# Attention heads: weight splits queued behind the scores' exponentials, and the remainders of eleven weights made by an accumulating transfer

## Chip, cores and metric

One core of one Trainium2 chip runs the kernel. The metric is the device time of one execution in microseconds (us). The engines are TensorE (PE; its weight loads are shown as PEld), VectorE (DVE), ScalarE (ACT), GpSimd (POOL) and SyncE (SP), each with a queue of its own that is worked off in order.

## Reference

Two layers on a sequence of 512 tokens of width 1024: a Mamba-2 layer with an FFN, then multi-head attention with an FFN. The change is in the attention layer, eight heads over four blocks of 128 queries:

```python
c_q = rms_norm(h @ q_down, q_norm_g)
q = (c_q @ q_up).reshape(b, s, MLA_N_HEADS, MLA_NOPE + MLA_ROPE)
...
scores = (jnp.einsum('bqhd,bkhd->bhqk', qn, k_nope)
          + jnp.einsum('bqhr,bkr->bhqk', qr, k_rope)).astype(jnp.float32) * scale
...
scores = jnp.where(key_idx[None, :] <= q_idx[:, None], scores, -jnp.inf)
p = jax.nn.softmax(scores, axis=-1).astype(v.dtype)
return jnp.einsum('bhqk,bkhd->bqhd', p, v)
...
return o @ out_proj
```

## The kernel before

**Splits.** Every product is made in fp32 accuracy from two parts of each operand: a rounded part and the remainder. `WStream` streams all weights in the order of use. `load` (line 54) puts one weight tile into a buffer `wst`; `_split` makes `wh` from it by a copy on ScalarE (line 96) and `wl = wst - wh` by a subtraction on VectorE (line 97). A product takes three passes: `wh` with the rounded activations, `wl` with them, `wh` with their remainders. `wh` and `wl` have six buffers each, `wst` six. `ahead(i, most)` splits up to `most` tiles beyond item i. The attention's items are, at the end of the list, `hw` 0 to 7 (one tile of 640 columns per head, q and k weights together) and `ow` 0 to 7 (output weights, 1024 columns).

**One pass of the head loop** (in `mla`, for h from 0 to 7) issues, in this order of code: `qk(h + 1)`, the q and k products of the next head, whose two banks ScalarE casts (line 1235, `qT`, `kT`) and VectorE takes the remainders of (line 1236); for every second head `qk_rope(h + 1)`, four transposes into one bank, which gives `qrT` of two heads, `qrT0` and `qrT1` below (cast at line 1251, remainder at line 1252; the second cast waits for the first remainder); one split; `pv(h - 1)`, whose bank becomes `oT` (lines 1307, 1308); `ptrans(h)`, ten transposes of the probabilities `E` into four banks, from which `PT` is cast (line 1290) and its remainder taken (line 1291); one more split; `scores(h + 1)`, four blocks i = 0 to 3 of 128, 256, 384 and 512 columns, each with five products in one bank (line 1265), the mask (1273), the maximum (1275), the exponential on ScalarE (1277), and the reciprocal and scaling on VectorE (1278, 1279). "Head h" is below the stretch that begins with `qk(h)` and ends with `scores(h)`, so that it holds `pv(h - 2)` and `ptrans(h - 1)`, and the exponentials that ScalarE runs during it are those of head h - 1.

**What sets the order.** A scheduler orders the queues of all engines but SP from the order of the code and its own estimate of times; `tc.issue_after(x)` keeps what is issued inside it behind x. The result is fixed when the kernel is built, and the chip works each queue off in that order. The eight PSUM banks (`k.bank()`) go round: a bank is given again eight requests later, and TensorE's first product into it waits until the last engine has read it. In a head with `qk_rope` the requests are q, k, rope, pv, four of `ptrans`, four of `scores`: block 2 of the scores gets the bank of `qk_rope`, block 3 that of `pv`. In a head without it block 3 gets the bank of `pv` likewise, and block 2 that of k.

Of the kernel before, what the change touches and what calls it, by code (L numbers as in the profile page):

```python
# [13 lines left out]
AF = mybir.ActivationFunctionType  # L14
ALU = mybir.AluOpType
# [3 lines left out]
P = 128  # L19
# [9 lines left out]


class WStream:

# [41 lines left out]
    def _split(self, nst=None):  # L76
        nc = self.k.nc
        i = self.split
        f, kind, part = (self.items[i][1:] + (None, None))[:3]
        if kind == "=":  # L80
            self.st[i] = self.st["+"]
        elif i not in self.st:
            self.load(i)
        s = self.st.pop(i)
        if kind == "+":
            self.st["+"] = s
            r = self.sums[part]
            nc.vector.tensor_tensor(r[:, :f], r[:, :f], s[:, :f], op=ALU.add)  # L88
            s = r
        elif kind == "-":  # L90
            nc.vector.tensor_tensor(s[:, :f], self.sums[part][:, :f], s[:, :f], op=ALU.subtract)
        if kind not in ("r", "a", "+"):
            self.out -= 1
        h = self.k.wh.tile([P, 1024], F32R, name="wh")
        l = self.k.wl.tile([P, 1024], F32R, name="wl")
        nc.scalar.copy(h[:, :f], s[:, :f])  # L96
        nc.vector.tensor_tensor(l[:, :f], s[:, :f], h[:, :f], op=ALU.subtract)  # L97
        self.w[i] = (h, l)
        self.split += 1
        self.fill(nst)  # L100
# [956 lines left out]
AH, QR, KVR, RD = 8, 384, 256, 64  # L1057
SCALE = (128 + 64) ** -0.5
# [6 lines left out]
def mla_items(dw, vw, rw, hw, ow):  # L1065

    it = [(dw[j], 1024) for j in range(4)] + [(dw[j][:, :768], 768) for j in (4, 5)]
    rv = rw.rearrange("(k p) n -> p k n", p=P)
    it += [(rv[:, 0:2, :], 1024), (rv[:, 2:3, :], 512)]
    vv = vw.rearrange("(k p) n -> p k n", p=P)  # L1070
    it += [(vv[:, :, hf * 512:(hf + 1) * 512], 1024) for hf in range(2)]
    it += [(hw[h], 640) for h in range(AH)]
    it += [(ow[j * P:(j + 1) * P, :], 1024) for j in range(AH)]
    return it


# [45 lines left out]
def mla(k, ws, base, ngp, gb):  # L1122
    nc, tc = k.nc, k.tc
    with ExitStack() as cx:
# [16 lines left out]
        n = [base]  # L1141
# [84 lines left out]
        def qk(h, off=0):  # L1226
            S = H.setdefault(h, {})
            w = [v[:, :640].rearrange("p (k m) -> p k m", k=5) for v in ws.get(n[0] + off, 0)]
            bq, bk = k.bank(), k.bank()
            k.mm_a(bq, [v[:, 0:3] for v in w], cT[:3], slice(0, SEQ))  # L1230
            k.mm_a(bk, [v[:, 3:5] for v in w], cT[3:], slice(0, SEQ))

            for nm, b, sc in (("q", bq, SCALE), ("k", bk, 1.0)):
                t = one.tile([P, 2, SEQ], F32R, name=f"{nm}T")
                a = nc.scalar.activation(t[:, 0], b, AF.Copy, scale=sc)
                d = nc.vector.scalar_tensor_tensor(t[:, 1], b, sc, t[:, 0], op0=ALU.mult, op1=ALU.subtract)
                S[nm] = t
            if not off:
                ws.retire(n[0])
                n[0] += 1  # L1240
            return a, d

        def qk_rope(h):
            if h % 2 == 0:
                b = k.bank()
                for i in range(NT):
                    nc.tensor.transpose(b[:, i * P:(i + 1) * P], qr[:, i, h * RD:(h + 2) * RD], k.ident)
                for e in range(2):
                    t = one.tile([P, SEQ], F32R, name=f"qrT{e}")
                    s = b[e * RD:(e + 1) * RD, :]  # L1250
                    a = nc.scalar.activation(t[:RD], s, AF.Copy, scale=SCALE)
                    d = nc.vector.scalar_tensor_tensor(t[RD:], s, SCALE, t[:RD], op0=ALU.mult, op1=ALU.subtract)
                    H.setdefault(h + e, {})["r"] = t
                return a, d

        def scores(h):
            S = H[h]
            S["E"] = []
            for i in range(NT):
                b = k.bank()  # L1260
                L = (i + 1) * P
                qs = slice(i * P, L)
                o = b[:, :L]
                q, kk, r = S["q"], S["k"], S["r"]
                mm = lambda l, m, s, e: nc.tensor.matmul(o, l, m, start=s, stop=e, skip_group_check=True)  # L1265
                mm(q[:, 0, qs], kk[:, 0, :L], True, False)
                mm(q[:, 0, qs], kk[:, 1, :L], False, False)
                mm(q[:, 1, qs], kk[:, 0, :L], False, False)
                mm(r[:, qs], ka[:, :L], False, False)
                mm(r[:, qs], kb[:, :L], False, True)  # L1270

                d = b[:, qs]
                nc.vector.tensor_tensor(d, d, mask, op=ALU.add)
                m = two.tile([P, 4], F32, name="smx", bufs=4)
                nc.vector.tensor_reduce(m[:, 0:1], o, axis=AX.X, op=ALU.max, negate=True)  # L1275
                e = one.tile([P, L], F32, name=f"E{i}")
                nc.scalar.activation(e, o, AF.Exp, bias=m[:, 0:1], accum_out=m[:, 1:2])
                nc.vector.reciprocal(m[:, 2:3], m[:, 1:2])
                nc.vector.tensor_scalar(e, e, m[:, 2:3], None, op0=ALU.mult)  # L1279
                S["E"].append(e)  # L1280

        def ptrans(h):
            S = H[h]
            S["P"] = []
            for j in range(NT):
                b = k.bank()
                for i in range(j, NT):
                    nc.tensor.transpose(b[:, i * P:(i + 1) * P], S["E"][i][:, j * P:(j + 1) * P], k.ident)
                t = one.tile([P, 2, SEQ - j * P], F32R, name=f"PT{j}")
                a = nc.scalar.copy(t[:, 0], b[:, j * P:])  # L1290
                d = nc.vector.tensor_tensor(t[:, 1], b[:, j * P:], t[:, 0], op=ALU.subtract)  # L1291
                S["P"].append(t)
            return a, d

        def pv(h):
            S = H.pop(h)
# [54 lines left out]
        n[0] += 3  # L1351
        for h in range(AH):
            if h + 1 < AH:

                ends = qk(h + 1)
                a, d = qk_rope(h + 1) or ends
                with tc.issue_after(a.ins), tc.issue_after(d.ins):
                    ws.ahead(n[0], most=1)
            else:
                k.load_ln(gb)  # L1360
                out_piece(0, 2, 0, ALPHA, False)
            if h:
                pv(h - 1)
            a, d = ptrans(h)
            if h + 1 < AH:
                with tc.issue_after(a.ins), tc.issue_after(d.ins):
                    ws.ahead(n[0], most=1)
            if h + 1 < AH:
                scores(h + 1)
        for i in range(1, NT):  # L1370
            out_piece(0, 2, i, ALPHA, False)
        pv(AH - 1)
# [90 lines left out]
```

## Time and profile before

| | us |
|---|---|
| median of 3 runs | 1312.35 (1311.97 to 1312.97) |
| the profiled execution's own time | 1311.7 |
| its span, first to last instruction | 1310.0 |
| busy in the span: PE, PEld, DVE | 1299.5, 1098.9, 1020.6 |
| busy in the span: ACT, POOL | 636.0, 93.1 |

TensorE is busy nearly everywhere by this table, but a product that waits inside its pipeline counts as busy, so stalls of some tenths of a microsecond are read from the waits and from the starts of its instructions. The granted clock of TensorE was 0.998 of full speed (the upper level, 2.4 GHz) over the span.

### The profile page before, as it was taken

The page shows a single profiled execution, that of the slowest core. Times are in us where ns is not written, and L with a number is a line of the kernel's source. Part 1 is how long each engine was busy: PE and PEld are TensorE (multiplying, and loading weights), DVE is VectorE, ACT ScalarE, POOL GpSimd, SP SyncE. Part 2 cuts the span into 40 slices and gives each one's busy share as a digit, 9 for nine tenths or more (in the row PEclk, how much of TensorE's full clock was granted, in tenths as well). Part 3 has the DMA queues.
Part 4 walks back from the last instruction along what each step waited for, and adds up shares of the span by engine and source line. Part 5 has one row for each costly group of instructions (what it writes and reads, how often), then busy time and mean ns, then how long its engine had stood idle before and what let it go on. Part 6 is the DMA issues. An engine that isn't in the chain of part 4 may idle for free.

```text
span 1310.0 us, 17422 instructions
## 1 busy us (share of the span) xinstructions
PE 1299.5 (99%) x6666; PEld 1098.9 (84%) x6666; DVE 1020.6 (78%) x1581; ACT 636.0 (49%) x1029; POOL 93.1 (7%) x96
## 2 busy tenths in 40 slices
PE   9999999999999999999999999999999999999997
PEld 8888888888888988888888899888898888888886
DVE  7888888797798868866766876898587686667587
ACT  6765555455453544444443434665254444444341
POOL 0111011011011001100000012000100010000000
PEclk9999999999999999999999999999999999999999
DMA  8423322313410433352311822121144227323251
GB/s 297 179 113 129 113 88 90 132 58 133 161 65 10 171 129 81 80 207 98 123 58 31 254 81 62 71 107 49 35 149 135 79 35 213 130 97 105 41 161 65
DMA packets 49779, 144.59 MB, mean 110 GB/s; under 512 B 5312, under 2 KB 6336, under 8 KB 48416
## 3 DMA queue, kind: packets, MB, share of 16 engines
q1 hardware_dynamic: 44480, 133.57, 28.8%
q0 software_dynamic: 5072, 9.77, 4.4%
q8 instruction: 52, 0.85, 0.3%
q14 instruction: 31, 0.25, 0.1%
q10 hardware_dynamic: 144, 0.15, 0.0%
HBM read 141.30 MB, written 2.16 MB: 110 GB/s over the span
## 4 chain that ended last, share of the span: by engine, by line
PE 95%; DVE 4%; ACT 1%; issue 0%; DVEq 0%; ACTq 0%
PE ps L159 57%; PE ps L165 10%; PE ps L167 10%; PE ps L166 10%; PE ps L803 1%; PE ps L915 1%; PE ps L811 1%; PE ps L274 1%; PE ps L792 1%; PE ps L742 1%; PE ps L1265 1%; DVE wl L97 1%; DVE PT L1291 1%; PE ps L770 1%; DVE E L1279 0%; DVE smx L1275 0%
## 5 line engine op out<-in xcount | busy, mean ns | idle before, releaser
L159 PE MATMUL ps<-ht,wh 128*128 128x512 f32 (+1 forms) x2256 | 517.0, 379 | 0.0
L159 PEld LDWEIGHTS ps<-ht,wh 128*128 128x128 f32 x2256 | 408.1, 188 | 79.7 <-issue 1.4
L97 DVE TENSOR_TENSOR wl<-wst,wh 128x1024 fp32r<-128x1024 f32 (+3 forms) x222 | 256.3, 1169 | 44.2 <-ACT wh L96 43.3
L96 ACT CAST wh<-wst 128x1024 fp32r<-128x1024 f32 (+3 forms) x222 | 218.8, 995 | 114.3 <-PE ps L167 62.3
L159 PE MATMUL ps<-ht,wl 128*128 128x512 f32 (+1 forms) x1128 | 266.6, 378 | 0.0
L159 PEld LDWEIGHTS ps<-ht,wl 128*128 128x128 f32 x1128 | 205.2, 188 | 39.6
L328 DVE SCALAR_TENSOR_TENSOR acc<-ps,cw,acc 128x511 f32<-128x511 f32 x88 | 65.7, 747 | 80.0 <-ACT acc L327 80.0
L165 PE MATMUL ps<-wh,gt 128*128 128x512 f32 (+1 forms) x320 | 123.7, 387 | 0.0
L167 PE MATMUL ps<-wh,gt 128*128 128x512 f32 (+1 forms) x320 | 123.6, 386 | 0.0
L166 PE MATMUL ps<-wl,gt 128*128 128x512 f32 (+1 forms) x320 | 123.6, 386 | 0.0
L340 ACT CAST gt<-acc 128x512 fp32r<-128x512 f32 (+1 forms) x80 | 44.0, 571 | 102.0 <-DVE acc L333 99.3
L657 DVE SCALAR_TENSOR_TENSOR cv<-ps,cw,cv 128x511 f32<-128x511 f32 (+2 forms) x96 | 71.3, 746 | 26.8 <-ACT cv L655 25.9
L327 ACT ACTIVATE acc<-ps,cw 128x512 f32<-128x512 f32 x88 | 68.3, 776 | 29.5 <-PE ps L159 29.4
L167 PEld LDWEIGHTS ps<-wh,gt 128*128 128x128 f32 x320 | 60.1, 188 | 12.3
L332 ACT ACTIVATE acc<-acc 128x512 f32<-128x512 f32 x44 | 27.8, 632 | 87.6 <-DVE acc L329 87.5
L165 PEld LDWEIGHTS ps<-wh,gt 128*128 128x128 f32 x320 | 60.1, 188 | 12.1
L166 PEld LDWEIGHTS ps<-wl,gt 128*128 128x128 f32 x320 | 60.1, 188 | 12.1
L329 DVE SCALAR_TENSOR_TENSOR acc<-ps,cw,acc 128x510 f32<-128x510 f32 x88 | 65.8, 748 | 2.5
L52 POOL DMA_DIRECT2D rs<-in_down_dram x24 | 25.4, 1058 | 572.7 <-DVE wl L97 572.7
L96 ACT CAST wh<-rs 128x1024 fp32r<-128x1024 f32 (+1 forms) x48 | 39.9, 834 | 46.4 <-DVE rs L88 27.1
L341 DVE TENSOR_TENSOR gt<-acc,gt 128x512 fp32r<-128x512 f32 (+1 forms) x80 | 48.8, 627 | 13.5 <-ACT gt L340 13.5
L387 DVE SCALAR_TENSOR_TENSOR h<-h,ps 128x512 f32<-128x512 f32 x56 | 37.6, 686 | 26.0 <-PE ps L167 26.0
(242 smaller groups left out, 1744.7 us busy)
## 6 DMA issues: line engine op xcount, KB each, us to landing
wst<-in_up_dram SPq DMA_DIRECT2D x88, 512.0 KB, 3.5
wst<-in_xbc_dram SPq DMA_DIRECT2D x32, 512.0 KB, 6.0
wst<-in_down_dram SPq DMA_DIRECT2D x26, 512.0 KB, 5.5
W<-cumd SPq DMA_DIRECT2D x8, 1024.0 KB, 4.6
wst<-in_sow_dram SPq DMA_DIRECT2D x16, 512.0 KB, 3.6
wst<-in_zw_dram SPq DMA_DIRECT2D x14, 512.0 KB, 6.1
rs<-in_down_dram POOLq DMA_DIRECT2D x12, 512.0 KB, 6.9
wst<-in_down_dram SPq DMA_DIRECT2D x18, 256.0 KB, 2.6
```

The lines of the kernel that those rows point to most:

```text
L96: nc.scalar.copy(h[:, :f], s[:, :f])
L97: nc.vector.tensor_tensor(l[:, :f], s[:, :f], h[:, :f], op=ALU.subtract)
L159: nc.tensor.matmul(out, w[:, k, :], xts[k][:, x, ts], start=first and p == 0 and k == 0, stop=last and p == 2 and k == nk - 1, skip_group_ ...
L165: nc.tensor.matmul(out, xt[:, 0, tsl], wh, start=start, stop=False, skip_group_check=True)
L166: nc.tensor.matmul(out, xt[:, 0, tsl], wl, start=False, stop=False, skip_group_check=True)
L167: nc.tensor.matmul(out, xt[:, 1, tsl], wh, start=False, stop=stop, skip_group_check=True)
L327: nc.scalar.activation(a, b, AF.Identity, bias=cw[:, ch, 3:4], scale=cw[:, ch, 2:3])
L328: nc.vector.scalar_tensor_tensor(a[:, 1:], b[:, :SEQ - 1], cw[:, ch, 1:2], a[:, 1:], op0=ALU.mult, op1=ALU.add)
L329: nc.vector.scalar_tensor_tensor(a[:, 2:], b[:, :SEQ - 2], cw[:, ch, 0:1], a[:, 2:], op0=ALU.mult, op1=ALU.add)
L340: k.nc.scalar.copy(dst[:, 0, :], src)
L341: k.nc.vector.tensor_tensor(dst[:, 1, :], src, dst[:, 0, :], op=ALU.subtract)
L657: nc.vector.scalar_tensor_tensor(t[:, d:], b[:, :SEQ - d], cw[:, ch, 3 - d:4 - d], t[:, d:], op0=ALU.mult, op1=ALU.add)
```

## The change

Eleven items get the kind "d": `hw` 1 to 7 and `ow` 0 to 3. For these VectorE no longer subtracts. ScalarE writes `-wst` into `wl`, rounded as `wh` is, and GpSimd issues a transfer within SBUF that adds `wst` to it. The splits of the head loop move: instead of one behind the casts of `qk` and `qk_rope` and one behind those of `ptrans`, both stand behind `scores(h + 1)`, after its last exponential and its last scaling.

```diff
         nc.scalar.copy(h[:, :f], s[:, :f])
-        nc.vector.tensor_tensor(l[:, :f], s[:, :f], h[:, :f], op=ALU.subtract)
+        if kind == "d":
+            nc.scalar.activation(l[:, :f], s[:, :f], AF.Copy, scale=-1.0)
+            nc.gpsimd.dma_start(l[:, :f], s[:, :f], accum_op=ALU.add)
+        else:
+            nc.vector.tensor_tensor(l[:, :f], s[:, :f], h[:, :f], op=ALU.subtract)
...
-    it += [(hw[h], 640) for h in range(AH)]
-    it += [(ow[j * P:(j + 1) * P, :], 1024) for j in range(AH)]
+    it += [(hw[h], 640) + ("d",) * (h > 0) for h in range(AH)]
+    it += [(ow[j * P:(j + 1) * P, :], 1024) + ("d",) * (j < 4) for j in range(AH)]
...
             if h + 1 < AH:
-
-                ends = qk(h + 1)
-                a, d = qk_rope(h + 1) or ends
-                with tc.issue_after(a.ins), tc.issue_after(d.ins):
-                    ws.ahead(n[0], most=1)
+                qk(h + 1)
+                qk_rope(h + 1)
...
-            a, d = ptrans(h)
+            ptrans(h)
             if h + 1 < AH:
+
+                a, d = scores(h + 1)
                 with tc.issue_after(a.ins), tc.issue_after(d.ins):
-                    ws.ahead(n[0], most=1)
-            if h + 1 < AH:
-                scores(h + 1)
+                    ws.ahead(n[0], most=2)
```

What this does to the queues is seen in their rows (line, operation, out<-in, shape; lines of the changed kernel stand up to five higher; the numbers of `E`, `PT` and `qrT` tell the tiles apart). On ScalarE in head 4, from the last exponential of head 3 on, there stood before (`qrT_7709` and `qrT_7712` are the two of one `qk_rope`):

```order
L1277 ACTIVATE E_7677,smx<-ps,smx 128x512
L1235 ACTIVATE kT<-ps 128x512
L1251 ACTIVATE qrT_7709<-ps 64x512
L1251 ACTIVATE qrT_7712<-ps 64x512
L96 CAST wh<-wst 128x1024
L1307 CAST oT<-ps 128x512
L1290 CAST PT_7742<-ps 128x512
L1290 CAST PT_7749<-ps 128x384
```

In the changed kernel there stands at the same place, from the exponential of the same block on:

```order
L1280 ACTIVATE E_7678,smx<-ps,smx 128x512
L97 CAST wh<-wst 128x1024
L99 ACTIVATE wl<-wst 128x1024
L1240 ACTIVATE kT<-ps 128x512
L1255 ACTIVATE qrT_7717<-ps 64x512
L1310 CAST oT<-ps 128x512
L1294 CAST PT_7744<-ps 128x512
L1294 CAST PT_7751<-ps 128x384
L1255 ACTIVATE qrT_7720<-ps 64x512
```

The split, now two instructions, has moved from behind `qrT` to in front of `kT`, and the second cast of `qrT` to behind two casts of `PT`; VectorE's remainders follow in the same order. Head 6 reads like head 4. In head 3, which has no `qk_rope`, ScalarE has two splits at that place in the changed kernel:

```order
L1240 ACTIVATE qT<-ps 128x512
L1280 ACTIVATE E_7534,smx<-ps,smx 128x384
L1280 ACTIVATE E_7547,smx<-ps,smx 128x512
L97 CAST wh<-wst 128x640
L99 ACTIVATE wl<-wst 128x640
L97 CAST wh<-wst 128x640
L99 ACTIVATE wl<-wst 128x640
L1240 ACTIVATE kT<-ps 128x512
L1310 CAST oT<-ps 128x512
```

Four instructions stand there between the exponential and `kT`. In head 2 there are four as well, and `qT`, `kT`, `qrT` come behind them; in heads 5 and 7 there are two of 1024 columns ahead of `kT`. On GpSimd the additions for the rotary part of q (line 1119 before) had nothing between them; now the queue holds there:

```order
L1176 TENSOR_TENSOR css<-css,mhalf 128x2
L100 DMA wl<-wst 128x640
L1124 TENSOR_TENSOR qr<-qr,rtmp 128x512 x3
L100 DMA wl<-wst 128x640
L1124 TENSOR_TENSOR qr<-qr,rtmp 128x512
L100 DMA wl<-wst 128x640 x5
L100 DMA wl<-wst 128x1024 x4
```

The transfer of `hw` 2 stands ahead of the last addition, which the first `qk_rope` needs; the other transfers have only later work of GpSimd behind them. The queue of SP is the same row for row, and outside the attention layer so are those of the other engines.

## Rows read from the trace of the kernel before

**Rows 1.** The page of the profile: busy time of each engine over the span (share, instructions), and the chain of work that ended last, by engine.
```profile
PE 1299.5 (99%) x6666; PEld 1098.9 (84%) x6666; DVE 1020.6 (78%) x1581; ACT 636.0 (49%) x1029; POOL 93.1 (7%) x96
...
PE 95%; DVE 4%; ACT 1%; issue 0%; DVEq 0%; ACTq 0%
```

**Rows 2.** Busy time of each engine in two stretches, the head loop (837 to 907 us) and part of the output projection behind it. Columns: stretch, its length, busy us (and instructions) of PE, PEld, DVE, ACT, POOL, then the clock granted to TensorE as a share of full speed, the DMA share and GB/s.
```profile
917.00:935.00 18.00, 18.00 (x87) 15.13 (x86) 8.35 (x16) 2.62 (x4) 1.69 (x2) 1.00 0.19 64
837.00:907.00 70.00, 68.43 (x404) 60.23 (x402) 66.72 (x177) 46.16 (x119) 0.00 (x0) 1.00 0.25 91
```

**Rows 3.** The chain that ended last, 850 to 872 us: its shares by engine and line in this stretch, and two of its pieces (start, us, what).
```profile
by line: DVE wl L97 14.1%; DVE PT L1291 11.9%; DVE E L1279 9.2%; DVE smx L1275 8.7%; ACT E L1277 8.5%; issue 7.1%; PE ps L1265 6.5%; DVE oT L1308 5.9%; DVE ps L1273 5.5%; ACT wh L96 4.3%; DVE smx L1278 3.9%; DVE qrT L1252 3.2%; DVE kT L1236
...
868.37 1.23 DVE wl L97
...
869.62 0.70 DVE oT L1308
```

**Rows 4.** Who waited for whom, 832 to 908 us, the rows of TensorE's weight loads (PEld): us in total, times, longest.
```profile
PEld ps L1265 <- DVE oT L1308: 1.7, 3, 0.7
PEld ps L1288 <- DVE E L1279: 1.4, 2, 0.9
...
PEld ps L1265 <- DVE kT L1236: 0.3, 1, 0.3
```

**Rows 5.** TensorE's instructions in order of time, from the work of heads 2 to 6: start, us, engine, line, operation, out<-in, shape, count (of like instructions in a row), and in brackets idle time before and what ended it. L159 is the q and k product of a head, L1265 its scores.
```profile
840.59 0.86 PE L159 MATMUL ps<-cT,wh 128*128 128x512 f32 x3
...
861.07 0.86 PE L159 MATMUL ps<-cT,wh 128*128 128x512 f32 x3
...
867.84 0.53 PE L1265 MATMUL ps<-kT,qT 128*128 128x128 f32 x3
868.21 0.27 PE L1265 MATMUL ps<-ka,qrT 128*128 128x128 f32 x1
...
869.08 0.69 PE L1265 MATMUL ps<-kT,qT 128*128 128x384 f32 x3
...
870.37 0.96 PE L1265 MATMUL ps<-kT,qT 128*128 128x512 f32 x3 [0.25 <-DVE oT L1308]
871.16 0.40 PE L1265 MATMUL ps<-ka,qrT 128*128 128x512 f32 x1
...
871.63 0.85 PE L159 MATMUL ps<-cT,wh 128*128 128x512 f32 x3
...
877.93 0.53 PE L1265 MATMUL ps<-kT,qT 128*128 128x128 f32 x3
...
880.05 0.86 PE L1265 MATMUL ps<-kT,qT 128*128 128x512 f32 x3
880.75 0.39 PE L1265 MATMUL ps<-ka,qrT 128*128 128x512 f32 x1
```

**Rows 6.** ScalarE's instructions in order of time, same columns; two splits ahead of the head loop, and then the exponentials of 512 columns at the end of `scores(1)` and of `scores(3)` with casts behind them.
```profile
820.90 1.41 ACT L96 CAST wh<-wst 128x640 fp32r<-128x640 f32 x2 [0.81 <-PE ps L167]
...
843.96 0.69 ACT L1277 ACTIVATE E<-ps,smx 128x512 f32<-128x512 f32 x1
...
863.96 0.69 ACT L1277 ACTIVATE E<-ps,smx 128x512 f32<-128x512 f32 x1
...
864.69 0.60 ACT L1235 ACTIVATE kT<-ps 128x512 fp32r<-128x512 f32 x1
865.19 0.58 ACT L1251 ACTIVATE qrT<-ps 64x512 fp32r<-64x512 f32 x1
...
873.94 0.60 ACT L1235 ACTIVATE qT<-ps 128x512 fp32r<-128x512 f32 x1 [0.43 <-PE ps L159]
...
876.27 1.04 ACT L96 CAST wh<-wst 128x1024 fp32r<-128x1024 f32 x1
877.21 0.60 ACT L1307 CAST oT<-ps 128x512 fp32r<-128x512 f32 x1
```

**Rows 7.** Instructions of the head loop (832 to 908 us) grouped by line and shape, VectorE first, then ScalarE ("..." between): line, engine, operation, names, shapes, count | busy us, mean ns of one | idle us before.
```profile
L97 DVE TENSOR_TENSOR wl<-wst,wh 128x1024 fp32r<-128x1024 f32 x6 | 7.3, 1223 | 0.5 <-ACT wh L96 0.5
...
L1252 DVE SCALAR_TENSOR_TENSOR qrT<-ps,qrT 64x512 fp32r<-64x512 f32 x6 | 4.1, 689 | 1.4 <-ACT qrT L1251 1.3
...
L97 DVE TENSOR_TENSOR wl<-wst,wh 128x640 fp32r<-128x640 f32 x4 | 3.3, 822 | 0.0
...
L96 ACT CAST wh<-wst 128x1024 fp32r<-128x1024 f32 x6 | 6.2, 1044 | 0.0
...
L1290 ACT CAST PT<-ps 128x384 fp32r<-128x384 f32 x7 | 3.5, 498 | 0.0
...
L96 ACT CAST wh<-wst 128x640 fp32r<-128x640 f32 x4 | 3.0, 740 | 0.0
```

**Rows 8.** The FFN's accumulating transfers (line 52, into `rs` from DRAM), the only ones in the kernel before: issue time on GpSimd, and from issue to landing.
```profile
L52 POOL DMA_DIRECT2D rs<-in_down_dram x24: 860/1056/1407, 507.0 to 1258.0; - x24
...
DMA to landing us min/median/max: 4.0/6.7/9.8
```

**Rows 9.** GpSimd's additions for the rotary part of q (start, us), and below the "..." VectorE's two subtractions that ran beside the last of them.
```profile
811.65 2.56 POOL L1119 TENSOR_TENSOR qr<-qr,rtmp 128x512 f32<-128x512 f32 x2 [4.68 <-DVE qr L1118]
...
823.04 1.80 POOL L1119 TENSOR_TENSOR qr<-qr,rtmp 128x512 f32<-128x512 f32 x1 [5.52 <-DVE qr L1118]
...
822.88 2.64 DVE L97 TENSOR_TENSOR wl<-wst,wh 128x640 fp32r<-128x640 f32 x2
```

More of the change, by code (lines that the diff above doesn't have):

```diff
@@ L1234, in qk @@
                 t = one.tile([P, 2, SEQ], F32R, name=f"{nm}T")
-                a = nc.scalar.activation(t[:, 0], b, AF.Copy, scale=sc)
-                d = nc.vector.scalar_tensor_tensor(t[:, 1], b, sc, t[:, 0], op0=ALU.mult, op1=ALU.subtract)
+                nc.scalar.activation(t[:, 0], b, AF.Copy, scale=sc)
+                nc.vector.scalar_tensor_tensor(t[:, 1], b, sc, t[:, 0], op0=ALU.mult, op1=ALU.subtract)
                 S[nm] = t
@@ L1240, in qk @@
                 n[0] += 1
-            return a, d
         def qk_rope(h):
@@ L1250, in qk_rope @@
                     s = b[e * RD:(e + 1) * RD, :]
-                    a = nc.scalar.activation(t[:RD], s, AF.Copy, scale=SCALE)
-                    d = nc.vector.scalar_tensor_tensor(t[RD:], s, SCALE, t[:RD], op0=ALU.mult, op1=ALU.subtract)
+                    nc.scalar.activation(t[:RD], s, AF.Copy, scale=SCALE)
+                    nc.vector.scalar_tensor_tensor(t[RD:], s, SCALE, t[:RD], op0=ALU.mult, op1=ALU.subtract)
                     H.setdefault(h + e, {})["r"] = t
-                return a, d
         def scores(h):
@@ L1276, in scores @@
                 e = one.tile([P, L], F32, name=f"E{i}")
-                nc.scalar.activation(e, o, AF.Exp, bias=m[:, 0:1], accum_out=m[:, 1:2])
+                a = nc.scalar.activation(e, o, AF.Exp, bias=m[:, 0:1], accum_out=m[:, 1:2])
                 nc.vector.reciprocal(m[:, 2:3], m[:, 1:2])
-                nc.vector.tensor_scalar(e, e, m[:, 2:3], None, op0=ALU.mult)
+                d = nc.vector.tensor_scalar(e, e, m[:, 2:3], None, op0=ALU.mult)
                 S["E"].append(e)
+            return a, d
         def ptrans(h):
@@ L1289, in ptrans @@
                 t = one.tile([P, 2, SEQ - j * P], F32R, name=f"PT{j}")
-                a = nc.scalar.copy(t[:, 0], b[:, j * P:])
-                d = nc.vector.tensor_tensor(t[:, 1], b[:, j * P:], t[:, 0], op=ALU.subtract)
+                nc.scalar.copy(t[:, 0], b[:, j * P:])
+                nc.vector.tensor_tensor(t[:, 1], b[:, j * P:], t[:, 0], op=ALU.subtract)
                 S["P"].append(t)
-            return a, d
         def pv(h):
```

## The prediction

> **What bounds the kernel now.** The page comes first: TensorE is busy 99% of the span and holds 95% of the chain that ended last, VectorE only 4% of it [rows 1]. A change that spares VectorE work can therefore only pay in a stretch where TensorE waits for it. The stretches show where that is: in the head loop VectorE is busy 66.7 of 70 us and ScalarE 46.2, while right behind it TensorE is busy 18.00 of 18.00 us [rows 2]. In the loop the chain runs mostly through VectorE, and the largest single share, 14.1%, is the subtraction at line 97, which the change takes away; one of them stands directly ahead of the remainder of `oT` [rows 3]. How much TensorE loses by it is read from its weight loads, which wait before the products do: 1.7 us in three places for `oT`, 1.4 us in two for a scaled `E`, 0.3 us in one for `kT`, together 3.4 us in six stalls [rows 4]. So the gain is at most 3.4 us, and 0.3 of that, the wait for `kT` in head 1, comes right after its own casts and has no split in front of it.
>
> I count from a head's first q product, T. In head 4 T is 861.07; the scores begin at T+6.77 (867.84), their fourth product, which needs `qrT`, at T+7.14, block 2 at T+8.01 [rows 5]. In head 5, without `qk_rope`, T is 871.63 and the scores begin at T+6.30 [rows 5]; by head 4's spacing the second product, which needs the remainder of `kT`, follows 0.12 later, at T+6.42.
>
> **The change part by part.**
>
> *VectorE's relief.* Four subtractions of 640 columns (0.82 us each) and four of the six of 1024 (1.22) leave the loop [rows 7]: some 8 us, on an engine whose work then takes less time than TensorE's. The stalls for `oT` and `E` go: 3.1 us gained.
>
> *ScalarE's new work.* The negated copy is not in the trace. Its nearest row is the cast `wh`, same source, size and target: 0.740 us at 640 columns and 1.044 at 1024 [rows 7]; in a row the next instruction starts 0.94 after the start of the 1024 one (876.27 to 877.21) [rows 6], so 0.94, and 0.62 for 640 columns by the same overlap of 0.1. Scaling costs nothing over a cast: `kT`, a scaled copy, takes 0.60 and so does the cast `oT` of the same size; copies of that size follow each other by 0.5 (864.69 to 865.19) [rows 6]. I take the cast's price; the bounds are a tenth less and more for each instruction. ScalarE's total, 46.2 us and some 6.2 more (4 times 0.62, 4 times 0.94), still fits in 70. What matters is what the copies stand in front of.
>
> *The place.* In head 4 before, the exponential of 512 columns starts at T+2.89 (863.96), `kT` at T+3.62, the first `qrT` at T+4.12 [rows 6], so `kT` and its remainder are long ready at T+6.77. Now two halves of a 1024 split come between. With the exponential at the same T+2.9 (the scores that it waits for end at T, as before) the walk in heads 4 and 6 is:
> - ScalarE: split from T+3.6 to T+5.5; `kT` T+5.5, first `qrT` T+6.0, `oT` T+6.5, two casts of `PT` T+7.0 and T+7.5 (the second is a tenth shorter, 0.498 [rows 7]), second `qrT` T+7.8.
> - VectorE, 0.69 for a remainder [rows 7], next start 0.6 later: `kT` T+6.1, first `qrT` T+6.7 to T+7.4, `oT` T+7.3, `PT` T+7.9, second `qrT` T+8.5 to T+9.2.
> - TensorE wants the first `qrT` at T+7.14 and gets it at T+7.4: 0.25 lost. It then wants block 2 at T+8.26, but that block's bank is the one of `qk_rope`, read to the end at T+9.2: 0.9 lost. Together 1.15 per head.
>
> In heads 5 and 7 the remainder of `kT` ends at about T+6.7, and TensorE wants it at T+6.42: 0.3 each.
>
> Head 2 has four halves of 0.62. Its exponential started at 843.96 before [rows 6]; two subtractions of some 0.73 leave VectorE ahead of it, so about 842.5, free at 843.2. The four halves end at 845.6; then `qT`, `kT` 846.1, first `qrT` 846.6, `oT`, two `PT`, second `qrT` 848.5. VectorE ends the remainder of `kT` at 847.5, the first `qrT` at 848.2, the second near 850.0. T is 840.59 [rows 5], so TensorE wants the second product at 847.48, the fourth at 847.73 and block 2 at 848.60: lost 0.2, 0.3 and 0.95, 1.45 in all.
>
> In head 3 T moves to about 852.1. ScalarE's queue has `qT` ahead of the exponentials of 384 and 512 columns, and `qT` needs all of the q product: in head 5 it started at T+2.31 (873.94) [rows 6]. Then 854.4, the exponentials until 856.2, four halves until 858.6, `kT` 858.6 to 859.2, its remainder to 859.9. TensorE wants `kT` at 858.4: 0.85 until the cast is there, and after two products on it 0.4 more for the remainder, 1.25.
>
> *Starting again.* After a stall the three products of block 3 took from 870.37 to 871.16, 0.79; without one 880.05 to 880.75, 0.70 [rows 5]: 0.09 for each stall. The weight loads' 3.4 holds this already for the old ones, the new terms do not. Twelve stalls (head 1 one, 2 three, 3 two, 4 and 6 two each, 5 and 7 one each) make 1.1.
>
> *The transfers.* GpSimd has nothing in the head loop but these. The kernel's other accumulating transfers take 0.86 to 1.41 us to issue and land in 4.0 to 9.8 [rows 8]. The tightest are `hw` 2 (split where ScalarE did it before, from 820.90 [rows 6], so copied by 821.6; used in head 2's second pass, 840.59 plus three products) and `hw` 4 (copied by 844.4, used near 864.5): 19 and 20 us, twice the longest landing. So they cost nothing; a landing beyond 19 us would cost TensorE what is over. The issue for `hw` 2 stands ahead of GpSimd's last addition, but with a middle 1.06 [rows 8] it ends near 822.7, and that addition started at 823.04 [rows 9]; one that is late there would hold the first `qk_rope` by as much. The addition took 1.80 beside two subtractions (the two together 2.64 instead of 1.64), where two earlier ones took 2.56 [rows 9]; the subtractions are gone, so half a microsecond of room is gained.
>
> *The output projection.* Its `wh` and `wl` are made earlier than they are needed, and TensorE is full there [rows 2]: nothing.
>
> **Sum.** New stalls 0.3 + 1.45 + 1.25 + 1.15 + 0.3 + 1.15 + 0.3 = 5.9, starting again 1.1, old stalls -3.4: +3.6 us. It lies inside the span; on the profiled execution's own 1311.7 (a span of 1310.0 and 1.7 around it) that gives 1315.3. This execution lies 0.65 below the median 1312.35, so on the median the forecast is 1315.9.
>
> A tenth more or less on each copy of a split, `wh` and `wl` both, moves heads 2 and 3 by 0.4 and 4 to 7 by 0.2 each, 1.6 in all; the old stalls, where one cast of each head stands ahead of `oT`, move by some 0.4 with it: +2.4 to +4.8.
>
> **The rivals.**
> - *The gain comes* (faster). `kT` must be on ScalarE by about T+5.1 in the odd heads, and the second `qrT` off VectorE by T+8.0 in the even ones. That holds if the exponentials run 1.2 us earlier than T+2.9, since VectorE is freed. For it: VectorE loses a tenth of its work. Against: the last exponential waits for a maximum over the block of scores that TensorE ends at T, and TensorE does not bring that earlier. Time: -3.1, so 1309.2; half of it 1310.8.
> - *The even heads don't stall* (about the same): the second `qrT` gets off its bank in time. This decides at T+8.0, 1.2 before my walk has it. Heads 2, 4, 6 then lose 0.5, 0.25, 0.25, and the sum is 0.3 + 0.5 + 1.25 + 0.25 + 0.3 + 0.25 + 0.3 + 0.8 - 3.4 = +0.6: 1312.9.
> - *Late remainders* (slower still): a landing of 22 us makes head 2 or 4 wait 3 us more, 1318.9. Against it stand 9.8 us as the longest landing and a queue of transfers that has nothing else. The Trainium skill (SBUF — State Buffer, "A bandwidth-pool intuition that's wrong") speaks for it: GpSimd cannot write the descriptors of its transfers while VectorE holds the port that they share, and a transfer of some 620 ns alone took some 3100 ns beside a VectorE copy; by that, as an estimate, each landing is 2.5 us later, and the sum stays. VectorE and GpSimd did slow each other down here beside the last addition [rows 9]; no row shows it for an issue.
> - *The change does nothing*: the splits find ScalarE idle. Before, `kT` came straight behind the exponential (863.96 and 0.69 of it, then 864.69) [rows 6], so there is no idle time at that place. Time: 1312.35.
>
> **Numbers.** The walk as written 0.67, the gain 0.10, even heads without stall 0.13, late remainders 0.07, nothing 0.03. This kernel's measurement tells about 0.2%, 2.6 us, from no change. The walk's range crosses it at the lower end: about 0.54 of its 0.67 is slower; with the late remainders slower is 0.61, faster 0.08 (most of the gain's chance), same 0.31. The walk alone would be 1314.7 to 1317.2; the range for 8 in 10 reaches down to the second rival's case and a little below it, and up towards a late remainder: 1311.9 to 1318.2.
>
> **What would show it.** In the changed profile: line 97's subtractions gone from the head loop but for two of 1024; VectorE's busy time there down by some 8 us and ScalarE's up by 6; waits of TensorE for `oT` and `E` gone, and in their place waits for `kT` and `qrT` in heads 2 to 7, the longest, near 0.9, ahead of block 2 in heads 2, 4 and 6; the loop 3 to 4 us longer. The forecast is wrong if ScalarE reaches `kT` before T+5.1, if the second `qrT` is off its bank before T+8, or if TensorE waits for a transfer.

## The result, and the profile after

The changed kernel takes 1314.49 us (median of 22 runs, 1313.76 to 1315.23), the kernel before 1312.30 (22 runs, 1311.88 to 1312.97): a ratio of 1.0016, 95% interval 1.0010 to 1.0022. It is slower by 2.2 us. By the bound of 0.2% named in the prediction that is still "same", although the interval excludes a change of nothing. The profiled execution took 1314.57 us itself, with a span of 1312.9.

The page and the stretches that answer [rows 1, 2]:

```profile
PE 1300.8 (99%) x6666; PEld 1099.4 (84%) x6666; DVE 1010.9 (77%) x1570; ACT 643.3 (49%) x1040; POOL 102.0 (8%) x107
PE 96%; DVE 2%; ACT 1%; issue 0%; DMA 0%; SPq 0%; DVEq 0%; ACTq 0%
917.00:935.00 18.00, 18.00 (x85) 15.10 (x84) 9.02 (x16) 3.83 (x5) 1.70 (x2) 1.00 0.19 64
837.00:907.00 70.00, 67.15 (x391) 58.84 (x390) 55.99 (x161) 49.67 (x123) 6.86 (x8) 1.00 0.45 117
```

VectorE is busy 55.99 of 70 us in the loop instead of 66.72, and holds 2% of the chain instead of 4%. So it is relieved as meant. ScalarE went from 46.16 to 49.67, and TensorE, the engine that counts, is busy 1.28 us less of the same 70. The granted clock is at its full level in both kernels (1.00 in both stretches), so the loss is waiting. For whom, the waits of 832 to 912 us tell (they answer [rows 4]):

```profile
DVE kT L1241 <- ACT kT L1240: 9.6, 6, 2.2
PEld ps L1268 <- DVE kT L1241: 1.9, 4, 0.5
PEld ps L1268 <- ACT kT L1240: 1.8, 3, 0.9
PEld ps L1268 <- DVE qrT L1256: 1.0, 3, 0.4
```

No wait for `oT`, for `E` or for a transfer is left. In their place TensorE waits for `kT` and `qrT`, 4.7 us (0.3 of it in head 1, as before). VectorE, which has less to do, itself sits idle for 9.6 us until ScalarE has cast `kT`. Where that cast stands, ScalarE's timeline shows in head 4 (T, the start of its first q product, is 863.05) and head 5 (T 873.40); it answers [rows 6]:

```profile
865.31 0.60 ACT L1240 ACTIVATE qT<-ps 128x512 fp32r<-128x512 f32 x1 [0.16 <-PE ps L164]
865.80 0.68 ACT L1280 ACTIVATE E<-ps,smx 128x512 f32<-128x512 f32 x1
...
866.46 1.05 ACT L97 CAST wh<-wst 128x1024 fp32r<-128x1024 f32 x1
867.41 1.06 ACT L99 ACTIVATE wl<-wst 128x1024 fp32r<-128x1024 f32 x1
868.36 0.59 ACT L1240 ACTIVATE kT<-ps 128x512 fp32r<-128x512 f32 x1
...
877.01 0.69 ACT L1280 ACTIVATE E<-ps,smx 128x512 f32<-128x512 f32 x1
...
877.68 1.05 ACT L97 CAST wh<-wst 128x1024 fp32r<-128x1024 f32 x1
878.61 1.08 ACT L99 ACTIVATE wl<-wst 128x1024 fp32r<-128x1024 f32 x1
879.57 0.60 ACT L1240 ACTIVATE kT<-ps 128x512 fp32r<-128x512 f32 x1
```

And TensorE's, with the waits in brackets (it answers [rows 5]): the first row is the start of head 4, the next ones are its scores, the last two those of head 5.

```profile
863.05 0.86 PE L164 MATMUL ps<-cT,wh 128*128 128x512 f32 x3
...
870.45 0.33 PE L1268 MATMUL ps<-ka,qrT 128*128 128x128 f32 x1
...
871.38 0.69 PE L1268 MATMUL ps<-kT,qT 128*128 128x384 f32 x3
...
872.25 0.86 PE L1268 MATMUL ps<-kT,qT 128*128 128x512 f32 x3
...
873.40 0.86 PE L164 MATMUL ps<-cT,wh 128*128 128x512 f32 x3
...
880.23 0.33 PE L1268 MATMUL ps<-kT,qT 128*128 128x128 f32 x1 [0.27 <-ACT kT L1240]
880.96 0.44 PE L1268 MATMUL ps<-kT,qT 128*128 128x128 f32 x2 [0.40 <-DVE kT L1241]
```

In head 5 `kT` is cast at T+6.17 and both halves of it are waited for. In head 4 it is cast at T+5.31, and block 2 (384 columns) starts at T+8.33 with no wait at all. That second reading is against the forecast.

The clearest measure is the length of each head, from its first q product to that of the next. For the kernel before, the changed one and all experiments below (worked out from the starts in TensorE's timeline of each profiled execution; "out" runs from the first output product to the first one behind `ptrans(7)`; "loss" is the sum over the row less that of e3, in which TensorE waits for nothing in heads 2 to 7):

| kernel | head 2 | 3 | 4 | 5 | 6 | 7 | out | loss | median us |
|---|---|---|---|---|---|---|---|---|---|
| before | 10.03 | 10.45 | 10.56 | 9.58 | 10.63 | 9.99 | 6.15 | 2.9 | 1312.30 |
| changed | 10.74 | 10.97 | 10.35 | 10.72 | 10.41 | 10.67 | 5.63 | 5.0 | 1314.49 |
| e1 places only | 10.03 | 10.18 | 10.30 | 10.37 | 10.31 | 10.36 | 5.64 | 2.7 | 1312.02 |
| e2 transfers only | 10.34 | 9.57 | 11.28 | 9.89 | 11.17 | 10.18 | 5.92 | 3.9 | 1313.60 |
| e3 no copies | 10.04 | 9.59 | 10.04 | 9.56 | 10.03 | 9.60 | 5.62 | 0 | 1309.30 |
| e4 block 2 on rope's bank | 11.04 | 10.98 | 11.13 | 9.94 | 11.41 | 9.91 | 5.64 | 5.6 | 1315.12 |
| e5 no copies in 4, 6 | 10.74 | 10.99 | 10.03 | 10.42 | 10.03 | 10.28 | 5.63 | 3.6 | 1312.85 |
| e6 no copies in 5, 7 | 10.73 | 10.97 | 10.34 | 9.78 | 10.60 | 9.75 | 5.62 | 3.3 | 1312.73 |
| e7 GpSimd subtracts | 10.03 | 9.57 | 10.03 | 9.59 | 10.04 | 9.56 | 5.63 | 0 | 1310.45 |
| e8 split behind `kT` | 10.76 | 9.59 | 10.03 | 9.56 | 10.56 | 9.97 | 6.26 | 2.3 | 1311.68 |
| e9 e7 in the old places | 10.03 | 9.60 | 10.03 | 9.57 | 10.06 | 10.20 | 6.25 | 1.3 | 1311.90 |
| e10 e7 in the loop only | 10.04 | 9.59 | 10.04 | 9.56 | 10.03 | 9.60 | 5.62 | 0 | 1309.40 |

From before to changed the loop gains 2.1 us of loss, and the medians differ by 2.2: the whole result lies in the head loop. The span of the profiled execution grew by 2.9, but 0.76 of that was there before the loop's first head began (its first q product starts at 833.26 instead of 832.50). The medians of the table are 1309.4 plus the loss, within 0.3 us, for all but e7 and e9, which lose 1.1 us elsewhere (below).

### The profile page after: what moved, and what is told of

Same layout as the page of the kernel before. It is cut to its first block, busy times and chain, and to the rows that moved or that the text cites. A ratio compares the mean times of both kernels' runs of the same rounds, so it can differ in the third digit from the quotient of the medians.

```text
span 1312.9 us, 17445 instructions
## 1 busy us (share of the span) xinstructions
PE 1300.8 (99%) x6666; PEld 1099.4 (84%) x6666; DVE 1010.9 (77%) x1570; ACT 643.3 (49%) x1040; POOL 102.0 (8%) x107
## 4 chain that ended last, share of the span: by engine, by line
PE 96%; DVE 2%; ACT 1%; issue 0%; DMA 0%; SPq 0%; DVEq 0%; ACTq 0%
PE ps L164 57%; PE ps L170 10%; PE ps L172 10%; PE ps L171 10%; PE ps L1268 1%; PE ps L808 1%; PE ps L816 1%; PE ps L279 1%; PE ps L1305 1%; PE ps L797 1%; PE ps L747 1%; PE ps L920 1%; PE ps L775 1%; DMA xst<-in_xT_dram 0%; PE ps L1292 0%
## 5 line engine op out<-in xcount | busy, mean ns | idle before, releaser
L102 DVE TENSOR_TENSOR wl<-wst,wh 128x1024 fp32r<-128x1024 f32 (+3 forms) x211 | 244.6, 1174 | 43.2 <-ACT wh L97 42.1
```

## The experiments

Theory A is the forecast's: what counts is the split work that stands on ScalarE between the last exponential of a head and the cast of `kT`, because scores, maximum, exponential, split, `kT` and the next scores form one chain.

**e1: the places without the transfers.**

```diff
-    it += [(hw[h], 640) + ("d",) * (h > 0) for h in range(AH)]
-    it += [(ow[j * P:(j + 1) * P, :], 1024) + ("d",) * (j < 4) for j in range(AH)]
+    it += [(hw[h], 640) for h in range(AH)]
+    it += [(ow[j * P:(j + 1) * P, :], 1024) for j in range(AH)]
```

> The changed places (both splits behind the scores' exponentials), but every wl by VectorE's subtraction: no negated copy, no accumulating transfer in the loop. Theory A (what counts is the split work that stands on ScalarE between the last exponential and the cast of kT): only the casts wh are left there, so kT is reached 0.62 to 1.24 us earlier than in the changed kernel; but the subtractions stand on VectorE ahead of the remainder of kT, so waits of TensorE for kT of 0.5 to 0.6 us stay in heads 3, 5 and 7 and of 0.2 to 0.3 for the first qrT in 4 and 6, about 2.5 us of stalls in all: 1311 to 1312, about 1 us under before and 3 under the changed kernel. Theory B (the places cost, whoever makes wl): as the changed kernel, 1314 to 1315.

Measured: 1312.02 us, ratio to before 0.9997 (0.9988 to 1.0006), loss 2.7. The waits:

```profile
PEld ps L1268 <- DVE kT L1241: 2.3, 4, 0.7
PEld ps L1268 <- DVE qrT L1256: 0.4, 2, 0.2
```

The sizes are close to A's (2.5 us forecast in all), the time is at the upper end of its range, and theory B falls. The new places alone are worth nothing and cost nothing against before; 2.5 us of the changed kernel's time belong to its new way of making `wl`.

**e2: the transfers without the places.** Against the kernel before; the places are its own.

```diff
-        nc.vector.tensor_tensor(l[:, :f], s[:, :f], h[:, :f], op=ALU.subtract)
+        if kind == "d":
+            nc.scalar.activation(l[:, :f], s[:, :f], AF.Copy, scale=-1.0)
+            nc.gpsimd.dma_start(l[:, :f], s[:, :f], accum_op=ALU.add)
+        else:
+            nc.vector.tensor_tensor(l[:, :f], s[:, :f], h[:, :f], op=ALU.subtract)
...
-    it += [(hw[h], 640) for h in range(AH)]
-    it += [(ow[j * P:(j + 1) * P, :], 1024) for j in range(AH)]
+    it += [(hw[h], 640) + ("d",) * (h > 0) for h in range(AH)]
+    it += [(ow[j * P:(j + 1) * P, :], 1024) + ("d",) * (j < 4) for j in range(AH)]
```

> The kernel before with its old places (one split behind the casts of qk and qk_rope, one behind those of ptrans), but with the negated copy and the accumulating transfer. Theory A: the 1.0 us copies now stand on ScalarE ahead of the cast of oT, so the waits for oT before block 3 in heads 4 and 6 grow from 0.4 to 0.6 to 1.0 to 1.2 us each, while VectorE's relief takes the waits for E in heads 3 and 7; together 3.5 to 4 us of stalls against 3.3: 1312 to 1313.5. Theory C (VectorE is what bounds the loop, and sparing it is a gain where the place is right): the stalls fall to under 1.5 us, 1310 or less. Theory D (the transfers themselves cost): 1314 or more, with waits of TensorE for wl.

Measured: 1313.60 us, 0.1 over A's range, ratio 1.0009 (1.0000 to 1.0018), loss 3.9. ScalarE in head 4, then TensorE's block 3:

```profile
867.97 1.03 ACT L96 CAST wh<-wst 128x1024 fp32r<-128x1024 f32 x1
868.90 1.06 ACT L98 ACTIVATE wl<-wst 128x1024 fp32r<-128x1024 f32 x1
869.99 0.59 ACT L1311 CAST oT<-ps 128x512 fp32r<-128x512 f32 x1
...
871.35 0.96 PE L1269 MATMUL ps<-kT,qT 128*128 128x512 f32 x3 [0.98 <-DVE oT L1312]
```

As A has it: the copy now delays `oT` instead of `kT`, and head 4 grows from 10.56 to 11.28 us, head 6 from 10.63 to 11.17. VectorE's relief shows in head 3, whose wait for a scaled `E` is gone (10.45 to 9.57), but the whole is a loss, against theory C. There is no wait for a transfer.

**e3: the copies away, the transfers kept.**

```diff
         if kind == "d":
-            nc.scalar.activation(l[:, :f], s[:, :f], AF.Copy, scale=-1.0)
-            nc.gpsimd.dma_start(l[:, :f], s[:, :f], accum_op=ALU.add)
+            nc.gpsimd.dma_start(l[:, :f], s[:, :f])
```

> The changed kernel without the negated copies: wl is filled by a plain transfer of wst instead of an accumulating one, so the remainders of these weights are left out of the product (wl holds the whole weight). ScalarE loses eleven copies, six or more of them in the loop; VectorE's work, the places and the transfers' number and sizes stay. Theory A: kT comes 0.95 to 1.25 us earlier in each head, all stalls of heads 2 to 7 go, 5 us less than the changed kernel: 1309 to 1310. Theory D (transfers, or descriptors written beside a busy VectorE): unchanged, 1314 to 1315.

Measured: 1309.30 us, ratio to before 0.9980 (0.9971 to 0.9989). One wait of TensorE is left in the loop, that of head 1:

```profile
PEld ps L1267 <- DVE kT L1240: 0.3, 1, 0.3
```

This is the cleanest cut. With ScalarE's copies gone and everything else in place 5 us go, of the 6.2 at which the prediction priced the eight copies in the loop. These transfers cost nothing that shows, so theory D falls. They are plain ones; that the accumulating ones cost nothing either is read from the changed kernel, where TensorE never waits for `wl`, and from e10 below, which has no such transfers at all and takes the same time.

**e4: block 2 on the bank that the forecast gave it.**

```diff
                     H.setdefault(h + e, {})["r"] = t
+                if h:
+                    H[h]["b2"] = b
...
-                b = k.bank()
+                b = S["b2"] if i == 2 and "b2" in S else k.bank()
```

> The changed kernel with one thing fixed: in heads 2, 4 and 6 block 2 of the scores is written into the bank of qk_rope, as the forecast had assumed it. If the forecast's walk failed in the bank alone, block 2 waits 0.7 to 0.9 us for the second qrT in heads 4 and 6 (and as much in head 2) and everything else stays: 1316 to 1317. If the heads are tied to each other through ScalarE and VectorE (mask, maximum, exponential, split, kT, scores), the wait appears in the even heads and is given back in the odd ones, whose own wait for kT falls from 1.1 to some 0.4 us: within 0.5 us of the changed kernel, 1314 to 1315.

Measured: 1315.12 us, ratio 1.0020 (1.0012 to 1.0029); against the changed kernel +0.6, just over the second theory's half microsecond and far from the first theory's 1.5 to 2.5. TensorE in head 4, and ScalarE in head 5 (T 874.38):

```profile
872.70 0.79 PE L1270 MATMUL ps<-kT,qT 128*128 128x384 f32 x3 [0.49 <-DVE qrT L1256]
...
877.21 0.69 ACT L1282 ACTIVATE E<-ps,smx 128x512 f32<-128x512 f32 x1
...
879.77 0.60 ACT L1240 ACTIVATE kT<-ps 128x512 fp32r<-128x512 f32 x1
```

The wait appears, and with it heads 4 and 5 take 11.13 and 9.94 us, where the changed kernel has 10.35 and 10.72: 21.07 together in both. For heads 6 and 7 it is 21.32 and 21.08, for 2 and 3 22.02 and 21.71. In head 5 the exponential starts at T+2.83 and `kT` at T+5.39, the forecast's T+2.9 and T+5.5. What head 4 loses at block 2 (0.78) head 5 gives back whole, and head 7 gives back 0.76 of the 1.00 of head 6; of the 0.30 of head 2 head 3 gives back nothing. (The scheduler also put some of block 3's products ahead of block 2 in heads 2 and 4, so the bracket shows less than the loss.)

**e5 and e6: the copies away in the even heads alone, and in the odd ones alone.** Output weights 0 and 2 are split in heads 4 and 6, 1 and 3 in heads 5 and 7. The edit of e5; e6 has (1, 3) for (0, 2).

```diff
+        elif kind == "p":
+            nc.gpsimd.dma_start(l[:, :f], s[:, :f])
...
-    it += [(ow[j * P:(j + 1) * P, :], 1024) + ("d",) * (j < 4) for j in range(AH)]
+    it += [(ow[j * P:(j + 1) * P, :], 1024) + (("p",) if j in (0, 2) else ("d",)) * (j < 4) for j in range(AH)]
```

> The changed kernel with the negated copy taken away only for the two output weights that are split in heads 4 and 6 (their wl is filled by a plain transfer, so these two remainders are left out of the product). The odd heads keep their own copy. Theory A1 (a head's loss is the whole chain from its own T: what VectorE still has to do when the scores end, maximum, exponential, split, kT): the even heads stop stalling, and in heads 5 and 7 the masks come earlier, so that the exponential of 512 columns starts near T+3.1 instead of T+3.6 and their stall falls from 1.1 to about 0.5 to 0.7 although their own copies stay. Heads 4 to 7 together lose 1.0 to 1.4 instead of 2.9 us: 1312.5 to 1313. Theory A2 (each head pays for its own copy alone): heads 4 and 6 fall from 0.35 to 0, heads 5 and 7 stay at 1.1: 1313.7.

> The counterpart: the negated copy taken away only for the two output weights that are split in heads 5 and 7 (these two remainders are left out of the product). Theory A1: kT comes 0.95 earlier in heads 5 and 7, whose stalls fall from 1.1 to under 0.2, and heads 4 and 6 keep 0.3 to 0.5: heads 4 to 7 lose 0.7 to 1.1 instead of 2.9 us: 1312 to 1312.7. Theory A2: heads 5 and 7 fall by 0.95 each, heads 4 and 6 stay at 0.35: the same here, so that this run tells how the copy of an odd head is priced and e5 tells the theories apart.

Measured: e5 1312.85 us, ratio 1.0003 (0.9993 to 1.0012); e6 1312.73 us, ratio 1.0003 (0.9994 to 1.0012). Over e3's lengths heads 4 to 7 lose 2.9 us in the changed kernel, in e5 0 + 0.86 + 0 + 0.68 = 1.5, in e6 0.30 + 0.22 + 0.57 + 0.15 = 1.2, each a tenth or two above A1's range. In e5 the odd heads, whose own work is unchanged, fall from 1.16 and 1.07 to 0.86 and 0.68 (A2 had them stay), because their exponential starts at T+3.29 in head 5 (T 872.84) instead of T+3.61 (ScalarE's timeline of e5):

```profile
876.13 0.69 ACT L1282 ACTIVATE E<-ps,smx 128x512 f32<-128x512 f32 x1
...
878.69 0.60 ACT L1242 ACTIVATE kT<-ps 128x512 fp32r<-128x512 f32 x1
```

So 0.30 of head 5's 1.16 and 0.39 of head 7's 1.07 came over from the even head ahead of it. Its own copy counts for more: without it (e6) 0.94 and 0.92 go. The two overlap, since together they exceed the loss.

**e7: GpSimd subtracts.**

```diff
         if kind == "d":
-            nc.scalar.activation(l[:, :f], s[:, :f], AF.Copy, scale=-1.0)
-            nc.gpsimd.dma_start(l[:, :f], s[:, :f], accum_op=ALU.add)
+            nc.gpsimd.tensor_tensor(l[:, :f], s[:, :f], h[:, :f], op=ALU.subtract)
```

> The changed places, with these weights' wl made by a subtraction on GpSimd instead of the negated copy and the accumulating transfer: ScalarE keeps the casts wh alone, VectorE stays relieved. The price of the subtraction is not in the traces; the nearest row is GpSimd's qr addition of 512 columns, 1.27 to 2.56 us, so 2.5 to 5 for 1024 columns against 19 us until it is used. Theory A (only ScalarE's queue ahead of kT counts): as the kernel without the copies, 1309 to 1309.6. Theory P (GpSimd and VectorE slow each other on the memory port that the qr additions showed, 0.5 us for each subtraction beside an addition): VectorE's masks and maxima come up to 0.5 us later in each head and some of the waits come back, 1310 to 1312.

Measured: 1310.45 us, ratio 0.9987 (0.9978 to 0.9996). In the loop TensorE waits for nothing from head 2 on, and the VectorE instructions that run beside a subtraction of GpSimd there, all of them remainders read out of PSUM, are no longer than in e3 (that of `oT` 690 ns in both): nothing of theory P shows there. But the median is 1.15 above e3's and above A's range, and the wait behind that stands ahead of the loop. GpSimd's timeline there, and TensorE's weight loads' wait between 820 and 832 us:

```profile
821.91 3.09 POOL L99 TENSOR_TENSOR wl<-wst,wh 128x640 fp32r<-128x640 f32 x2 [4.18 <-ACT wh L97]
824.97 1.26 POOL L1123 TENSOR_TENSOR qr<-qr,rtmp 128x512 f32<-128x512 f32 x1
```

```profile
PEld ps L1250 <- POOL qr L1123: 1.1, 1, 1.1
```

Two subtractions stand in front of the last `qr` addition, for which the transposes of `qk_rope(0)` wait.

**e8: both splits behind the cast of `kT`.** Against e1; `qk` returns its last cast and remainder.

```diff
-                qk(h + 1)
+                a, d = qk(h + 1)
                 qk_rope(h + 1)
+                with tc.issue_after(a.ins), tc.issue_after(d.ins):
+                    ws.ahead(n[0], most=2)
...
-                a, d = scores(h + 1)
-                with tc.issue_after(a.ins), tc.issue_after(d.ins):
-                    ws.ahead(n[0], most=2)
+                scores(h + 1)
```

> The changed places moved once more: both splits queued behind the cast of kT of qk (ahead of the casts of qrT and oT), every wl by VectorE's subtraction. Theory A: nothing of the split stands ahead of kT, so no wait for kT in heads 2 to 7; the wh cast and the subtraction stand ahead of oT and the scaled E instead, and about 2 us of stalls are left, for oT or E in heads 6 and 7: 1311 to 1311.5. Theory B (it is VectorE's load that counts, wherever its work is queued): as before, 1312.3.

Measured: 1311.68 us, ratio 0.9994 (0.9985 to 1.0003), loss 2.3, in heads 2, 6, 7 and "out". The waits of 832 to 912 us:

```profile
PEld ps L1269 <- PE ps L1269: 1.1, 2, 0.7
PEld ps L1293 <- DVE E L1283: 0.6, 1, 0.6
PEld ps L1269 <- DVE oT L1312: 0.4, 1, 0.4
PEld ps L1269 <- DVE kT L1241: 0.3, 1, 0.3
```

The wait for `kT` is gone from heads 2 to 7, as A has it, and those for `E` and `oT` are back. The first row, which the profile puts to TensorE itself, stands for block 2 of heads 2 and 6, by the waits of the products:

```profile
849.80 0.76 PE L1269 MATMUL ps<-kT,qT 128*128 128x384 f32 x3 [0.48 <-DVE qrT L1257]
...
889.56 0.76 PE L1269 MATMUL ps<-kT,qT 128*128 128x384 f32 x3 [0.29 <-DVE qrT L1257]
```

In the built program of e8 block 2 of heads 2, 4 and 6 has the bank of `qk_rope`, which it has not in e1. So e8 moved a bank along with the splits, and part of its 2.3 us belongs to that. The time lies between A's 1311.5 and B's 1312.3, nearer to A; the interval does not settle it.

**e9: GpSimd's subtraction in the old places.** Against e2.

```diff
-            nc.scalar.activation(l[:, :f], s[:, :f], AF.Copy, scale=-1.0)
-            nc.gpsimd.dma_start(l[:, :f], s[:, :f], accum_op=ALU.add)
+            nc.gpsimd.tensor_tensor(l[:, :f], s[:, :f], h[:, :f], op=ALU.subtract)
```

> The kernel before with its old places, and these weights' wl by GpSimd's subtraction, as in e7. Theory A: the casts wh alone stand ahead of the cast of oT, as in before, so waits for oT in head 7 of 0.5 to 0.9 us and for E ahead of the last transposes of 0.7 stay, VectorE's relief takes the others: about 1.9 us of stalls against 0.4 in e7 and 3.3 in before, 1311 to 1311.6: the new places are worth something where the remainders are made off both engines. If the places make no difference then: as e7, 1310 to 1310.6.

Measured: 1311.90 us, ratio 0.9998 (0.9989 to 1.0007). The waits in the loop are those that A named:

```profile
PEld ps L1268 <- DVE oT L1311: 0.7, 1, 0.7
PEld ps L1291 <- DVE E L1282: 0.7, 1, 0.7
PEld ps L1268 <- DVE kT L1239: 0.3, 1, 0.3
```

The time is 0.3 over A's range because of the same 1.1 us ahead of the loop as in e7, which I had not foreseen when I wrote it. So the new places are worth 1.3 us (e9's loss against none in e7) when GpSimd makes the remainders.

**e10: GpSimd only in the loop.** Against e7.

```diff
-    it += [(hw[h], 640) + ("d",) * (h > 0) for h in range(AH)]
+    it += [(hw[h], 640) + ("d",) * (h > 3) for h in range(AH)]
```

> As e7, but the three head weights that are split ahead of the head loop (hw 1 to 3) keep VectorE's subtraction; GpSimd makes wl only for hw 4 to 7 and output weights 0 to 3. In e7 two GpSimd subtractions of 640 columns (3.09 us) stood in front of the last qr addition, and TensorE waited 1.1 us for it ahead of the transposes of qk_rope(0). Theory: that wait goes, the loop stays free of stalls: 1.0 to 1.1 us under e7, 1309.3 to 1309.5. If the median of e7 lies above that of the kernel without the copies for another reason, it stays at 1310.4.

Measured: 1309.40 us (1309.13 to 1309.67), ratio to before 0.9978 (0.9969 to 0.9987). It is 2.8 us under the kernel before of the same runs (1312.18), and 5.1 under the changed kernel's median. Its loop:

```profile
837.00:907.00 70.00, 69.85 (x422) 62.82 (x421) 60.99 (x170) 48.83 (x124) 15.73 (x8) 1.00 0.22 77
```

TensorE is busy 69.85 of 70 us.

## Why the prediction came out as it did

The direction was right, and so was the cause: no wait is left for what VectorE had been late with, and new ones stand for `kT` and `qrT`, behind the split work on ScalarE. 1315.9 was forecast and 1314.49 came, inside the stated range but just under the 1314.7 to 1317.2 of the walk itself. By the bound of 0.2% "slower", which had a chance of 0.61, did not come, and "same", which had 0.31, did.

The sum had +3.6 us where the loop shows +2.1, and two of its terms were wrong, with opposite signs: the even heads by 3.0 us too much, heads 5 and 7 together by 1.45 too little. That the one made up for half of the other was luck for the forecast, though e4 shows that the two are tied (below). With the even heads put right alone the sum would have been the second rival's +0.6.

- **Relief of VectorE.** Right. It is 10.7 us in the window shown, since two subtractions of 1024 columns now run behind it (909 us) besides the 8 us that are gone. ScalarE's 3.5 instead of 6 has the same reason: two casts `wh` of 1.05 us moved behind 907. The old stalls that go were taken as 3.1 us; by head lengths they are 2.9. The 0.3 in head 1 stays.
- **Price of the negated copy.** Right: 0.735 to 0.747 us at 640 columns and 1.06 to 1.08 at 1024, against 0.74 and 1.044 of the cast.
- **Head 3.** Right: 1.25 and two restarts of 0.09, so 1.43 forecast, 1.38 measured.
- **The even heads: the step that failed.** "That block's bank is the one of `qk_rope`" is wrong for the changed kernel. I had counted banks by the order of the code, as the rule of eight requests above has it. The pool hands them out as they come free in the scheduler's order, and the built programs show what became of it. In the kernel before, block 2 has `qk_rope`'s bank in heads 4 and 6, but already not in head 2. In the changed kernel block 2 of heads 2, 4 and 6 waits for the remainder of `oT`, block 3 for that of the first `PT`, and `qk_rope`'s bank goes to the next head's q product. The trace agrees: block 2 started at 871.38, before VectorE had begun with the second remainder of `qrT` (its timeline in the changed kernel):

```profile
871.04 0.68 DVE L1295 TENSOR_TENSOR PT<-ps,PT 128x512 fp32r<-128x512 f32 x1
871.75 0.69 DVE L1256 SCALAR_TENSOR_TENSOR qrT<-ps,qrT 64x512 fp32r<-64x512 f32 x1
872.48 1.09 DVE L1295 TENSOR_TENSOR PT<-ps,PT 128x384 fp32r<-128x384 f32 x3
873.48 0.49 DVE L1276 TENSOR_TENSOR ps<-ps,cmask 128x128 f32<-128x128 f32 x2
```

  That remainder ended at T+9.4, even later than my T+9.2, and cost nothing. With restarts, heads 2, 4 and 6 were forecast at 1.72, 1.33 and 1.33 and came to 0.70, 0.31 and 0.38, which is nearly the walk without its block 2 (0.68, 0.34 and 0.34). e4, which gives block 2 the assumed bank, brings 1.00, 1.09 and 1.38: given its premise the walk comes near in heads 4 and 6 and is too high in head 2.
- **The odd heads: mis-sized.** 0.39 each was forecast for heads 5 and 7, 1.16 and 1.07 came. The walk put their last exponential at T+2.9, taken from head 4 of before. In the rows above VectorE comes to the masks of head 4's scores only at T+0.08 of head 5, behind the second `qrT` and three `PT`; maximum and exponential follow, the latter at T+3.61. The trace of the kernel before had shown it, had I read its head 5 (T 871.63): there the exponential starts at T+3.49 (ScalarE's timeline of before):

```profile
875.12 0.69 ACT L1277 ACTIVATE E<-ps,smx 128x512 f32<-128x512 f32 x1
```

  The two errors belong together. A stall at block 2 would have let VectorE catch up and made the odd head's exponential early (e4); without it the odd head pays. Heads 4 and 5, and 6 and 7, cost nearly the same together either way.
- **The rivals.** The second rival's condition (the second `qrT` off its bank by T+8) never came true, yet its even heads did, and its +0.6 fell short by what the odd heads paid. The gain of the first rival, 2.9 us, exists in full, but only where neither ScalarE nor VectorE makes a remainder ahead of `kT` (e3, e7, e10). Late remainders didn't come: landings of 3.5 to 6.4 us against 19 us of room. By the estimate worked out from the Trainium skill (SBUF — State Buffer, "A bandwidth-pool intuition that's wrong") each landing would be 2.5 us later beside VectorE. The trace doesn't show it: of the seven transfers of 640 columns the two issued while VectorE was idle (845.60 and 857.77) landed in 3.5 us, the five issued with VectorE at work in 3.5 to 4.4. "Nothing" falls with the 5 us that the copies cost. The transfers of `wl` in the changed kernel, issue time in ns and landing in us, min/median/max:

```profile
L100 POOL DMA_DIRECT2D wl<-wst x11: 851/860/934, 808.8 to 901.3; - x11
...
DMA to landing us min/median/max: 3.5/4.2/6.4
```

- **The last addition of GpSimd.** The issue for `hw` 2 ahead of it cost nothing, as forecast, and the addition took 1.27 us instead of 1.80 [rows 9]. The warning that whatever is late there holds the first `qk_rope` came true in e7.

## What to carry to other kernels

Moving work from the busiest helper engine to an idler one pays only if the new place in the queue is not ahead of what the bound engine waits for next: ScalarE had 20 us to spare in 70, and the copies still cost 5 us, because they stood between an exponential and `kT`. Before pricing a wait for a buffer, read from the built program or from the trace which buffer it is, since a pool's hand-out changes with the order of the work, and take offsets from the same kind of head, even or odd, not from its neighbour. When two engines share a closed chain, look for the third that has nothing to do: the same subtraction on GpSimd, in the loop alone, made both parts of the change pay.

## What the runs showed of the hardware

GpSimd's subtraction (e7, 800 to 915 us, grouped by shape: busy us, mean ns) takes 1.57 us at 640 columns and 2.39 at 1024, about twice VectorE's 0.82 and 1.22 [rows 7]:

```profile
L99 POOL TENSOR_TENSOR wl<-wst,wh 128x640 fp32r<-128x640 f32 x7 | 10.8, 1568 | 31.3 <-ACT wh L97 31.3
L99 POOL TENSOR_TENSOR wl<-wst,wh 128x1024 fp32r<-128x1024 f32 x4 | 9.6, 2394 | 29.3 <-ACT wh L97 16.9 <-PE ps L1250 12.4
```

In the loop of e7 it ran beside remainders that VectorE reads out of PSUM, and slowed none of them; it started only as a scaling of `E` ended, and never ran beside a VectorE subtraction with both operands in SBUF. Beside two of these GpSimd's last `qr` addition took 1.80 us (before [rows 9], and again in e10), and without them 1.26 to 1.28 (changed kernel, e3, e7). I had put the subtraction at 2.5 to 5 us at 1024 columns, having read the 2.56 us of [rows 9] as one addition; they are two.
